# Row sums of a 64 MiB tensor: two blocks of 112 and 16 rows a partition in place of four of 32

## The chip, the cores and the metric

The kernel runs on one core of one Trainium2 chip. The metric is the device time of one execution in microseconds (us). The profile's span is a little shorter than that time: about 1.8 us lie outside the span.

## The reference

```python
def setup_inputs():
    batch, seq, dim = 32, 512, 1024
    return {"x": np.random.randn(batch, seq, dim).astype(np.float32)}

def reference(x):
    return np.sum(x, axis=-1).astype(np.float32)
```

16,384 rows of 1,024 floats are summed. 67.1 MB come in, 64 KiB go out. Nothing is used twice.

## The kernel before

Each block of 128 x n rows is laid out so that a partition holds n consecutive rows. A load tile takes 16 rows a partition: 64 KiB in each of 128 partitions, 8 MiB in all, in one of three buffers. VectorE sums whole tiles. A finished block of 32 rows a partition is stored from ScalarE's queue. The last two tiles are tuned: ScalarE takes 6 rows of the seventh, and the eighth comes in ever smaller pieces, so that little is left to do when the last bytes land. The cut below leaves lines out at each `...`, and its comments are added here.

```python
BLOCKS = (32, 32, 32, 32)
G = 16
ACT_ROWS = 6
CUT = 640
...
    xpool = ctx.enter_context(tc.tile_pool(name="x", bufs=3))
...
    def block(r0, n):
        x_b = x_flat[r0 : r0 + P * n].rearrange("(p c) d -> p (c d)", p=P)
        out_b = out_flat[r0 : r0 + P * n].rearrange("(p c) -> p c", p=P)
        return x_b, out_b, rpool.tile([P, n], F32, name=f"res{r0}")
...
        while c < whole:
            m = min(G, whole - c)
            xt = xpool.tile([P, G * D], F32, tag="xt", name="xt")
            nc.sync.dma_start(out=xt[:, 0 : m * D], in_=x_b[:, c * D : (c + m) * D])
            a = ACT_ROWS if final and c + m == whole else 0
            rows_dve(xt, res, 0, m - a, c)             # VectorE, tensor_reduce
            rows_act(xt, res, m - a, a, c + m - a)     # ScalarE, one activation a row
            c += m
        if not final:
            nc.scalar.dma_start(out=out_b, in_=res)
...
    # the eighth tile: pieces of 8, 4, 2 and 1 rows, then 640 and 384 columns of the last row
    for i, k in zip(cuts, cuts[1:]):
        nc.sync.dma_start(out=xt[:, i * D : k * D], in_=x_b[:, (c + i) * D : (c + k) * D])
    last = (n - 1) * D
    nc.sync.dma_start(out=tail[:, 0:CUT], in_=x_b[:, last : last + CUT])
    nc.sync.dma_start(out=tail[:, CUT:D], in_=x_b[:, last + CUT : last + D])
... # VectorE and ScalarE share the pieces
    nc.sync.dma_start(out=out_b, in_=res)
```

Of the kernel before, what the change touches and what calls it, by code (L numbers as in the profile page):

```python
# [1 line left out]

# [4 lines left out]

F32 = mybir.dt.float32
ADD = mybir.AluOpType.add
COPY = mybir.ActivationFunctionType.Copy  # L10
X = mybir.AxisListType.X

BLOCKS = (32, 32, 32, 32)
G = 16
ACT_ROWS = 6
CUT = 640


@with_exitstack
def kernel(  # L20
    ctx: ExitStack,
    tc: tile.TileContext,
    x: bass.AP,
    out: bass.AP,
):
    nc = tc.nc
    P = nc.NUM_PARTITIONS

    x_flat = x.flatten_outer_dims()
    R, D = x_flat.shape  # L30
    C = R // P
    assert R % P == 0 and sum(BLOCKS) == C
    out_flat = out.rearrange("a (b c) -> (a b c)", c=1)

    xpool = ctx.enter_context(tc.tile_pool(name="x", bufs=3))
    rpool = ctx.enter_context(tc.tile_pool(name="res", bufs=1))
    tail = rpool.tile([P, D + 2], F32, name="tail")

    def rows_dve(xt, res, j, n, c):
        nc.vector.tensor_reduce(  # L40
            out=res[:, c : c + n],
            in_=xt[:, j * D : (j + n) * D].rearrange("p (j d) -> p j d", d=D),
            axis=X,
            op=ADD,
        )

    def sum_act(v, acc):
        nc.scalar.activation(out=v, in_=v, func=COPY, accum_out=acc)  # L48

    def rows_act(xt, res, j, n, c):  # L50
        for i in range(n):
            sum_act(xt[:, (j + i) * D : (j + i + 1) * D], res[:, c + i : c + i + 1])

    def row_pairs_dve(xt, res, j, c):
        h = D // 2
        a, b = xt[:, j * D : j * D + h], xt[:, j * D + h : (j + 1) * D]
        nc.vector.tensor_tensor_reduce(  # L57
            out=a, in0=a, in1=b, scale=1.0, scalar=0.0, op0=ADD, op1=ADD,
            accum_out=res[:, c : c + 1],
        )  # L60

    def block(r0, n):
        x_b = x_flat[r0 : r0 + P * n].rearrange("(p c) d -> p (c d)", p=P)
        out_b = out_flat[r0 : r0 + P * n].rearrange("(p c) -> p c", p=P)
        return x_b, out_b, rpool.tile([P, n], F32, name=f"res{r0}")

    r0 = 0
    for b, n in enumerate(BLOCKS):
        x_b, out_b, res = block(r0, n)
        r0 += P * n  # L70
        final = b == len(BLOCKS) - 1
        whole = n - G - (n % G if final and n % G else 0) if final else n
        c = 0
        while c < whole:
            m = min(G, whole - c)
            xt = xpool.tile([P, G * D], F32, tag="xt", name="xt")
            nc.sync.dma_start(out=xt[:, 0 : m * D], in_=x_b[:, c * D : (c + m) * D])
            a = ACT_ROWS if final and c + m == whole else 0
            rows_dve(xt, res, 0, m - a, c)
            rows_act(xt, res, m - a, a, c + m - a)  # L80
            c += m
        if not final:
            nc.scalar.dma_start(out=out_b, in_=res)

    xt = xpool.tile([P, G * D], F32, tag="xt", name="xt")
    first = n - c - 8
    cuts = [0, first, first + 4, first + 6, first + 7]
    for i, k in zip(cuts, cuts[1:]):
        nc.sync.dma_start(out=xt[:, i * D : k * D], in_=x_b[:, (c + i) * D : (c + k) * D])
    last = (n - 1) * D  # L90
    nc.sync.dma_start(out=tail[:, 0:CUT], in_=x_b[:, last : last + CUT])
    nc.sync.dma_start(out=tail[:, CUT:D], in_=x_b[:, last + CUT : last + D])

    for i, k in zip(cuts[:2], cuts[1:3]):
        h = (k - i + 1) // 2
        rows_dve(xt, res, i, h, c + i)
        rows_act(xt, res, i + h, k - i - h, c + i + h)
    i = cuts[2]
    rows_dve(xt, res, i, 1, c + i)
    rows_act(xt, res, i + 1, 1, c + i + 1)  # L100
    row_pairs_dve(xt, res, i + 2, c + i + 2)
    nc.vector.tensor_reduce(  # L102
        out=tail[:, D : D + 1], in_=tail[:, 0 : CUT // 2], axis=X, op=ADD
    )
    sum_act(tail[:, CUT // 2 : CUT], tail[:, D + 1 : D + 2])
    nc.vector.tensor_reduce(  # L106
        out=res[:, n - 1 : n], in_=tail[:, CUT : D + 2], axis=X, op=ADD
    )
    nc.sync.dma_start(out=out_b, in_=res)


# [1 line left out]
_INS = ['x']  # L113
_OUTS = [((32, 512), 'float32')]


# [23 lines left out]
```

## Time and profile before

| before | |
|---|---|
| time | 163.21 us (median of 3 timed runs, 163.21 to 163.22) |
| the profiled execution | 163.75 us, span 162.0 us |
| mean load rate over the span | 415 GB/s |
| VectorE busy | 76% of the span |
| a tile of 8 MiB | lands every 19.33 to 19.72 us |
| VectorE's sum of a tile | 17.22 us |

The timeline of before (start in us, duration in us, engine, line and operation, then in brackets how long the engine had been idle and what ended that; lines left out). SPq and ACTq are the queues of SyncE and ScalarE, L40 is VectorE's sum:

```profile
22.68 17.22 DVE L40 TENSOR_REDUCE res<-xt 128x16 f32<-128x16384 f32 x1 [22.68 <-DMA xt<-in_x_dram]
42.04 17.22 DVE L40 TENSOR_REDUCE res<-xt 128x16 f32<-128x16384 f32 x1 [2.14 <-DMA xt<-in_x_dram]
61.56 17.22 DVE L40 TENSOR_REDUCE res<-xt 128x16 f32<-128x16384 f32 x1 [2.30 <-DMA xt<-in_x_dram]
81.28 17.22 DVE L40 TENSOR_REDUCE res<-xt 128x16 f32<-128x16384 f32 x1 [2.50 <-DMA xt<-in_x_dram]
...
122.25 0.33 SPq L91 DMA_DIRECT2D tail<-in_x_dram  x1
...
137.69 1.28 ACT L48 ACT_TABLE_LOAD   x1 [137.69 <-DVE res L40]
139.34 1.06 ACT L48 ACTIVATE xt<-xt 128x1024 f32<-128x1024 f32 x1 [0.37 <-DMA xt<-in_x_dram]
139.34 18.46 DVE L40 TENSOR_REDUCE res<-xt 128x10 f32<-128x10240 f32 x4 [2.11 <-DMA xt<-in_x_dram]
...
149.09 1.06 ACT L48 ACTIVATE xt<-xt 128x1024 f32<-128x1024 f32 x1 [3.41 <-DMA xt<-in_x_dram]
...
158.58 0.47 ACT L48 ACTIVATE tail<-tail 128x320 f32<-128x320 f32 x1 [0.97 <-DMA tail<-in_x_dram]
158.58 0.49 DVE L102 TENSOR_REDUCE tail<-tail 128x1 f32<-128x320 f32 x1
```

VectorE waits for a load before every tile, so the start of a sum is the moment its tile landed. The kernel is a load stream with work hidden under it. From 139.34 us on VectorE has no gap until 158.55 us, and at 158.58 us the next-to-last piece of the input lands: in the tail the load stream and VectorE are tied.

The chain of waits of before, and its stores in the DMA view (KB each, us from issue to landing):

```profile
by line: DMA xt<-in_x_dram 39.1%; DMA tail<-in_x_dram 22.4%; DVE res L40 21.3%; DMA out_dram<-res 14.6%; DVE res L106 0.3%; ACT tail L48 0.3%; issue 0.1%; ACTq L135 0.1%
...
98.53 23.70 DMA out_dram<-res
122.23 0.02 issue
122.25 36.30 DMA tail<-in_x_dram
```

```profile
out_dram<-res ACTq DMA_DIRECT2D x3, 16.0 KB, 23.7
out_dram<-res SPq DMA_DIRECT2D x1, 16.0 KB, 1.4
```

A store is 14.6% of the critical chain. SyncE's queue had waited 2.6 us for this store before it issued the load at 122.25 us. The two share no tile; that they share a semaphore is the likely reason, and no view names it. That load lands 36.3 us later, because it stands behind other loads: it was issued far too early for the wait to matter. A chain of waits shows what was waited for last, not what an earlier end would bring.

A second source is used below, the trace's packet records: one entry with start, duration and size for each DMA packet. They are given in plain words and tables, as no view prints them one by one. A load packet is one partition's 64 KiB. Of the 896 in before, most took exactly 2.418 us. That is 65,536 B / 2.418 us = 27.1 GB/s for an engine and 434 GB/s for sixteen. The Trainium skill (DMA: Bandwidth & Descriptors, Bandwidth, "Where 436 GB/s comes from") gives 435.2 GB/s as the ceiling of the sixteen ports; this trace agrees to half a per cent. Eight such packets for each engine and tile are 19.34 us. The stream has no room below that.

### The profile page before, as it was taken

Reading aid. Unit: us, or ns where it says so; the run is one execution under the profiler, and the core shown is the slowest. Engines: PE = TensorE matmul, PEld = TensorE weight load, DVE = VectorE, ACT = ScalarE, POOL = GpSimd, SP = SyncE. Lnnn points to the kernel's source line nnn. Section 1 sums busy time; section 2 is a strip of 40 time slices with the busy share of each in tenths; the row PEclk is TensorE's granted clock in tenths of the full one; section 3 lists DMA queues with packets and bytes.
Section 4 is the critical chain, followed back from the end, with each engine's and each line's share of the span. In section 5 each row is a group of like instructions: output and inputs, shape, how many; then the busy total and the mean of one; then the engine's idle time right before and its main releaser. Section 6 shows DMA issues by size and latency. Waiting matters only on the chain.

```text
span 162.0 us, 116 instructions
## 1 busy us (share of the span) xinstructions
DVE 123.5 (76%) x14; ACT 15.8 (10%) x29; POOL 0.2 (0%) x4
## 2 busy tenths in 40 slices
DVE  0000039998699967999499994999949998599994
ACT  0000000000000000000000000000000000991881
POOL 0000000000000000000000000000000000000000
DMA  7979989989979969969959959969969959999991
GB/s 259 518 324 453 518 356 421 518 388 388 518 340 437 518 275 502 519 259 519 519 259 518 518 259 518 519 259 519 519 260 518 518 259 518 389 398 443 405 410 35
DMA packets 2448, 67.18 MB, mean 415 GB/s; under 512 B 784, under 2 KB 912, under 8 KB 1168
## 3 DMA queue, kind: packets, MB, share of 16 engines
q1 hardware_dynamic: 2016, 67.13, 96.6%
q10 hardware_dynamic: 432, 0.05, 0.2%
HBM read 67.11 MB, written 0.07 MB: 415 GB/s over the span
## 4 chain that ended last, share of the span: by engine, by line
DMA 76%; DVE 22%; ACT 0%; issue 0%; ACTq 0%
DMA xt<-in_x_dram 39%; DMA tail<-in_x_dram 22%; DVE res L40 21%; DMA out_dram<-res 15%; DVE res L106 0%; ACT tail L48 0%; ACTq L135 0%
## 5 line engine op out<-in xcount | busy, mean ns | idle before, releaser
L40 DVE TENSOR_REDUCE res<-xt 128x16 f32<-128x16384 f32 (+4 forms) x10 | 121.8, 12203 | 36.0 <-DMA xt<-in_x_dram 36.0
L48 ACT ACT_TABLE_LOAD x1 | 1.3, 1283 | 137.7 <-DVE res L40 137.7
L48 ACT ACTIVATE xt<-xt 128x1024 f32<-128x1024 f32 x13 | 13.6, 1045 | 4.7 <-DMA xt<-in_x_dram 4.7
L48 ACT ACTIVATION_READ_ACCUMULATOR xt<-xt 128x1 f32 x13 | 2.4, 186 | 0.0
L57 DVE CUSTOM_DVE_ANT_0 xt<-xt 128x512 f32<-128x512 f32 x1 | 0.7, 693 | 0.1
L106 DVE TENSOR_REDUCE res<-tail 128x1 f32<-128x386 f32 x1 | 0.6, 554 | 0.1
L48 ACT ACTIVATE tail<-tail 128x320 f32<-128x320 f32 x1 | 0.5, 469 | 1.0 <-DMA tail<-in_x_dram 1.0
L102 DVE TENSOR_REDUCE tail<-tail 128x1 f32<-128x320 f32 x1 | 0.5, 486 | 0.0
L48 ACT ACTIVATION_READ_ACCUMULATOR tail<-tail 128x1 f32 x1 | 0.2, 187 | 0.0
L124 POOL MEMSET const-bfloat16-1.0<- 128x1 bf16 x1 | 0.1, 102 | 0.0
L124 POOL MEMSET const-uint8-127<- 128x1 uint8 x1 | 0.1, 101 | 0.0
L124 POOL MEMSET const-float32-0.0<- 128x1 f32 x1 | 0.1, 99 | 0.2 <-issue 0.2
L124 POOL MEMSET const-float32-1.0<- 128x1 f32 x1 | 0.1, 98 | 0.0
L57 DVE DVE_READ_ACCUMULATOR2_ANT res<- 128x1 f32 x1 | 0.1, 83 | 0.0
## 6 DMA issues: line engine op xcount, KB each, us to landing
xt<-in_x_dram SPq DMA_DIRECT2D x1, 4096.0 KB, 31.2
xt<-in_x_dram SPq DMA_DIRECT2D x1, 2048.0 KB, 35.7
xt<-in_x_dram SPq DMA_DIRECT2D x1, 1024.0 KB, 37.7
xt<-in_x_dram SPq DMA_DIRECT2D x1, 512.0 KB, 38.5
tail<-in_x_dram SPq DMA_DIRECT2D x1, 320.0 KB, 36.3
tail<-in_x_dram SPq DMA_DIRECT2D x1, 192.0 KB, 36.4
xt<-in_x_dram SPq DMA_DIRECT2D x7, 41.2
out_dram<-res ACTq DMA_DIRECT2D x3, 16.0 KB, 23.7
```

The source lines that it names most:

```text
L40: nc.vector.tensor_reduce(out=res[:, c : c + n], in_=xt[:, j * D : (j + n) * D].rearrange("p (j d) -> p j d", d=D), axis=X, op=ADD,)
L48: nc.scalar.activation(out=v, in_=v, func=COPY, accum_out=acc)
L57: nc.vector.tensor_tensor_reduce(out=a, in0=a, in1=b, scale=1.0, scalar=0.0, op0=ADD, op1=ADD, accum_out=res[:, c : c + 1],)
L102: nc.vector.tensor_reduce(out=tail[:, D : D + 1], in_=tail[:, 0 : CUT // 2], axis=X, op=ADD)
L106: nc.vector.tensor_reduce(out=res[:, n - 1 : n], in_=tail[:, CUT : D + 2], axis=X, op=ADD)
L124: nc = _bacc.Bacc("TRN2", target_bir_lowering=False, num_devices=1)
```

## The change

The intent is to have fewer stores while loads run: one of 112 values a partition (448 B) and one of 16 at the end, in place of four of 32. Three things come with it. The store of the large block can go only after the seventh tile, near the end. It stands in ScalarE's queue in front of the tail's row sums. And the distance in memory between the rows of neighbouring partitions, the pitch, grows from 32 rows (128 KiB) to 112 rows (448 KiB), with 64 KiB for the last tile.

```diff
-BLOCKS = (32, 32, 32, 32)
+BLOCKS = (112, 16)
...
-        whole = n - G - (n % G if final and n % G else 0) if final else n
+        whole = n - G if final else n
...
-            a = ACT_ROWS if final and c + m == whole else 0
+            a = ACT_ROWS if done + c + m == full else 0
...
-    first = n - c - 8
-    cuts = [0, first, first + 4, first + 6, first + 7]
+    cuts = [0, 8, 12, 14, 15]
```

`done` counts the rows of earlier blocks and `full` is 128 - G. The helper that sums the last single row in pairs is rewritten and renamed, but emits the same instruction; the rest of the diff is bookkeeping.

More of the change, by code (lines that the diff above doesn't have):

```diff
@@ L52, in rows_act, with pairs_dve @@
             sum_act(xt[:, (j + i) * D : (j + i + 1) * D], res[:, c + i : c + i + 1])
-    def row_pairs_dve(xt, res, j, c):
-        h = D // 2
-        a, b = xt[:, j * D : j * D + h], xt[:, j * D + h : (j + 1) * D]
+    def pairs_dve(xt, a, b, first, acc):
+        h = (a + b) // 2
         nc.vector.tensor_tensor_reduce(
-            out=a, in0=a, in1=b, scale=1.0, scalar=0.0, op0=ADD, op1=ADD,
-            accum_out=res[:, c : c + 1],
+            out=xt[:, a:h], in0=xt[:, a:h], in1=xt[:, h:b], scale=1.0, scalar=first,
+            op0=ADD, op1=ADD, accum_out=acc,
         )
@@ L65, in block @@
         return x_b, out_b, rpool.tile([P, n], F32, name=f"res{r0}")
-    r0 = 0
+    full = C - G
+    done = 0
     for b, n in enumerate(BLOCKS):
-        x_b, out_b, res = block(r0, n)
-        r0 += P * n
+        x_b, out_b, res = block(done * P, n)
         final = b == len(BLOCKS) - 1
-        whole = n - G - (n % G if final and n % G else 0) if final else n
+        whole = n - G if final else n
         c = 0
@@ L83 @@
             nc.scalar.dma_start(out=out_b, in_=res)
+        done += n
     xt = xpool.tile([P, G * D], F32, tag="xt", name="xt")
-    first = n - c - 8
-    cuts = [0, first, first + 4, first + 6, first + 7]
+    cuts = [0, 8, 12, 14, 15]
     for i, k in zip(cuts, cuts[1:]):
@@ L100 @@
     rows_act(xt, res, i + 1, 1, c + i + 1)
-    row_pairs_dve(xt, res, i + 2, c + i + 2)
+    i += 2
+    pairs_dve(xt, i * D, (i + 1) * D, 0.0, res[:, c + i : c + i + 1])
     nc.vector.tensor_reduce(
```

## The prediction

> **What bounds the kernel now.** The load stream. The page's mean is 415 GB/s over the 162.0 us span. The timeline shows when each 8 MiB tile lands, by the start of the reduce that waits for it: 22.68, 42.04, 61.56, 81.28, 100.61, 120.01, 139.34 us, every 19.33 to 19.72 us. In the trace's packet records a 64 KiB load packet takes 2.418 us at best, so 8 packets per engine and tile need 19.34 us: the steady state has no slack to win. VectorE needs 17.22 us a tile and waits 2.1 to 2.5 us for each (timeline); the next load is always queued. Only the tail is tied: from the seventh landing (139.34) VectorE runs without a gap to 158.55, when the first tail piece lands (158.58).
>
> **What the change does.**
> 1. Removes two of three mid-kernel stores (issued near 59 and 98 us). On the DMA engines each is 128 packets of 128 B, 13 ns each in the packet records: 8 per engine, about 0.1 us; the tile interval with only a store extra was 19.40 against 19.33 us. The 23.7 us from issue to landing is turn-taking with 64 KiB load packets, as the Trainium skill (DMA: Bandwidth & Descriptors, Queues, rings and completion order) has it: engines alternate between queues packet by packet; 9 store packets behind 9 of 2.42 us make 21.8 us, which agrees. The store's share of the critical chain (15%) is a semaphore reuse by a load issued long before it was needed, so worth nothing. Gain: 0.15 to 0.2 us.
> 2. Moves the remaining store. It now waits for the seventh tile's reduce (landing + 10.82 us, about 150.1) and stands in ScalarE's in-order queue ahead of the four rows of the 4 MiB piece, which started at 149.09 before. ScalarE starts them at about 150.5 (issue 0.36 us), 1.4 us late. It had idle times of 0.61, 0.30 and 0.97 us (timeline) to come, so it ends the last row about 0.4 us before the tail piece lands. Cost: 0, with small slack.
> 3. Changes the address pitch between partitions of a load from 128 KiB to 448 KiB, and 64 KiB for the last tile. The intervals 19.52 and 19.72 us hold packets of 2.45 to 2.53 us; about 0.55 us lost, not tied to stores. The skill (same page, Latency and other measured facts) reports a loss for pitches of large powers of two; 448 KiB is none, so I expect no loss. No trace here shows it yet.
> 4. The final store shrinks from 128 to 64 B per partition: its 1.4 us to landing stays. The pair-sum helper is the same instruction. The activation table load (1.28 us) moves to the start, into idle time.
>
> **Critical path.** About 0.2 us of removed DMA time lies on it, plus or minus packet luck of 0.5 us.
>
> **Prediction.** 163.0 us, range 162.3 to 163.8. Faster by over 2%: 0.02; within 2%: 0.95; slower by over 2%: 0.03.
>
> **What would show it.** Landing intervals of 19.33 to 19.5 us for all tiles (1, 3); ScalarE starting its four rows at landing + 11.2 us and still waiting for the tail piece (2); the store landing by about 156 us.
>
> **What would make it wrong.** The new pitch slowing load packets above 2.5 us on average; ScalarE's late start ending past the tail piece's landing; the late store delaying the tail loads by over 1 us; a load waiting for the late store through a shared semaphore.

## The result

After takes 163.25 us (median of 4 runs, 163.07 to 163.32) against 163.22 us (163.21 to 163.27) for before in the same rounds. The ratio is 1.0, with a 95% interval of 0.9982 to 1.0017: the same. Ratios here and below are the mean time of one kernel's fast runs over that of the other's of the same rounds, so they are not quite the ratio of the medians that are quoted.

The timeline of after, the lines that answer to those of before:

```profile
22.61 17.22 DVE L40 TENSOR_REDUCE res<-xt 128x16 f32<-128x16384 f32 x1 [22.61 <-DMA xt<-in_x_dram]
41.96 17.22 DVE L40 TENSOR_REDUCE res<-xt 128x16 f32<-128x16384 f32 x1 [2.13 <-DMA xt<-in_x_dram]
61.31 17.22 DVE L40 TENSOR_REDUCE res<-xt 128x16 f32<-128x16384 f32 x1 [2.13 <-DMA xt<-in_x_dram]
80.65 17.22 DVE L40 TENSOR_REDUCE res<-xt 128x16 f32<-128x16384 f32 x1 [2.12 <-DMA xt<-in_x_dram]
...
119.08 0.45 SPq L90 DMA_DIRECT2D tail<-in_x_dram  x1
...
138.70 18.46 DVE L40 TENSOR_REDUCE res<-xt 128x10 f32<-128x10240 f32 x4 [2.13 <-DMA xt<-in_x_dram]
138.77 1.28 ACT L48 ACT_TABLE_LOAD   x1 [138.77 <-DMA xt<-in_x_dram]
140.06 1.06 ACT L48 ACTIVATE xt<-xt 128x1024 f32<-128x1024 f32 x1
...
149.61 0.37 ACTq L82 DMA_DIRECT2D out_dram<-res  x1
150.10 1.06 ACT L48 ACTIVATE xt<-xt 128x1024 f32<-128x1024 f32 x1 [3.70 <-DVE res L40]
...
157.33 0.69 DVE L56 CUSTOM_DVE_ANT_0 xt<-xt 128x512 f32<-128x512 f32 x1 [0.16 <-DMA xt<-in_x_dram]
...
158.03 0.47 ACT L48 ACTIVATE tail<-tail 128x320 f32<-128x320 f32 x1 [0.54 <-DMA tail<-in_x_dram]
```

Its chain of waits by line, and its stores in the DMA view:

```profile
by line: DMA xt<-in_x_dram 50.5%; DMA tail<-in_x_dram 24.1%; DVE res L40 21.3%; SPq L88 1.0%; DVE res L106 0.3%; ACT tail L48 0.3%; issue 0.3%; SPq L76 0.2%; ACTq L135 0.1%
```

```profile
out_dram<-res ACTq DMA_DIRECT2D x1, 56.0 KB, 6.5
out_dram<-res SPq DMA_DIRECT2D x1, 8.0 KB, 1.4
```

Four readings. The tiles land every 19.34 to 19.36 us, the floor that the packets set. The store has left the chain, the tail load goes out 3.2 us earlier, and the time is the same: those 14.6% were worth nothing. ScalarE now starts the rows of the 8-row piece at 150.10 us, after it issued the store, 11.40 us after the seventh landing; before it was 149.09 - 139.34 = 9.75 us. And the profile of after is 0.5 us shorter (161.5 against 162.0 us) where the timed runs are equal, so something in the profile of before is chance or a tail of its distribution.

To keep the parts apart, two stretches are compared from here on, both read from the timeline: from the first landing to the seventh (six tiles in steady flow), and from the seventh landing to the start of the sums over `tail`, when the piece of 640 columns has landed.

| | first to seventh landing | seventh landing to tail piece |
|---|---|---|
| before | 139.34 - 22.68 = 116.66 us | 158.58 - 139.34 = 19.24 us |
| after | 138.70 - 22.61 = 116.09 us | 158.03 - 138.70 = 19.33 us |

### The profile page after: what moved, and what is told of

Its sections match the earlier page's. It is cut to its first block, busy times and chain, and to the rows that moved or that the text cites. A ratio compares the mean times of both kernels' runs of the same rounds, so it can differ in the third digit from the quotient of the medians.

```text
span 161.5 us, 115 instructions
## 1 busy us (share of the span) xinstructions
DVE 123.5 (76%) x14; ACT 15.6 (10%) x29; POOL 0.2 (0%) x4
## 4 chain that ended last, share of the span: by engine, by line
DMA 75%; DVE 22%; SPq 1%; ACT 0%; issue 0%; ACTq 0%
DMA xt<-in_x_dram 51%; DMA tail<-in_x_dram 24%; DVE res L40 21%; SPq L88 1%; DVE res L106 0%; ACT tail L48 0%; SPq L76 0%; ACTq L135 0%
## 5 line engine op out<-in xcount | busy, mean ns | idle before, releaser
L48 ACT ACT_TABLE_LOAD x1 | 1.3, 1283 | 138.8 <-DMA xt<-in_x_dram 138.8
L56 DVE CUSTOM_DVE_ANT_0 xt<-xt 128x512 f32<-128x512 f32 x1 | 0.7, 691 | 0.2 <-DMA xt<-in_x_dram 0.2
L56 DVE DVE_READ_ACCUMULATOR2_ANT res<- 128x1 f32 x1 | 0.1, 81 | 0.0
```

The lines of the kernel that those rows point to most:

```text
L48: nc.scalar.activation(out=v, in_=v, func=COPY, accum_out=acc)
L56: nc.vector.tensor_tensor_reduce(out=xt[:, a:h], in0=xt[:, a:h], in1=xt[:, h:b], scale=1.0, scalar=first, op0=ADD, op1=ADD, accum_out=acc,)
```

## The experiments

Theory A is that of the prediction: the load stream alone sets the time, a mid-kernel store costs 0.1 us or less, the pitch costs nothing. The rivals: B, the pitch changes the load rate, and the profiled 0.5 us is real. C, the stores disturb the stream by 0.3 us or more each, and the tail gives that gain back. D, ScalarE, held up behind the late store, gives it back. Later a theory E came out of the second stretch: the late store's packets delay the tail loads among which they run. The twelve runs below were made on three chips, those of one group on the same chip with shared runs of before.

### The kernel before again (e1_before_again)

No edit.

> The kernel before, unchanged. Theory A (the load stream alone sets the time, a store costs about 0.1 us of DMA time, the pitch nothing): its timed runs are 163.2 us; the profile of before (162.0 us of span, 163.75 us) was one unlucky execution, so a second profile has a span near 161.4 us and tile intervals of 19.34 to 19.45 us. Rival B (the profiled 0.5 us between before and after is real: slow load packets belong to the 128 KiB pitch): the second profile again shows a span near 162.0 us and intervals of 19.5 to 19.7 us.

163.25 us (6 runs, 163.06 to 163.79), ratio to before 0.9999 (0.9980 to 1.0018). Its profiled execution took 163.06 us with a span of 161.3 us. Three of its lines, the first landing, the seventh and the tail piece:

```profile
22.50 17.22 DVE L40 TENSOR_REDUCE res<-xt 128x16 f32<-128x16384 f32 x1 [22.50 <-DMA xt<-in_x_dram]
...
138.68 18.46 DVE L40 TENSOR_REDUCE res<-xt 128x10 f32<-128x10240 f32 x4 [2.14 <-DMA xt<-in_x_dram]
...
157.89 0.47 ACT L48 ACTIVATE tail<-tail 128x320 f32<-128x320 f32 x1 [0.97 <-DMA tail<-in_x_dram]
```

The first stretch is 116.18 us and the second 19.21 us. So of the 0.57 us that before seemed to lose against after in steady flow, 0.48 us (116.66 - 116.18) belong to that one execution, and this profile is the fair one to compare with: after gains 0.09 us in the first stretch and loses 0.12 us in the second.

### No mid-kernel stores (e2_no_mid_stores)

```diff
-        if not final:
-            nc.scalar.dma_start(out=out_b, in_=res)
```

Three quarters of the output stay unwritten.

> The kernel before without its three mid-kernel stores (three quarters of the output stay unwritten: wrong on purpose). Theory A: 3 x 0.1 us less, 162.9 us, every tile interval 19.34 to 19.36 us. Rival C (stores disturb the load stream by 0.3 us or more each, and the change gave that gain back in its tail): 162.3 us or less.

163.29 us (6 runs, 163.16 to 163.55), ratio 0.9998 (0.9979 to 1.0017); stretches 116.16 and 19.22 us. Rival C falls: 0.9 us or more of gain would lie outside the interval. Theory A's 0.3 us fell short too: the point estimate is 0.0002 x 163.3 = 0.03 us. The interval is 0.3 us wide on either side, so 0.3 us is only just inside. Its intervals were 19.32 to 19.41 us, not all at the floor as expected: this profile (163.39 us) has some slow load packets, of which more below. So this run bounds the stores' worth and doesn't measure it.

### The pitch alone (e3_pitch_alone)

The kernel after, with results in tiles of 32 columns that are stored when they are full:

```diff
+            if c % 32 == 0:
+                part = rpool.tile([P, 32], F32, name=f"part{c}")
-            rows_dve(xt, res, 0, m - a, c)
-            rows_act(xt, res, m - a, a, c + m - a)
+            rows_dve(xt, part, 0, m - a, c % 32)
+            rows_act(xt, part, m - a, a, c % 32 + m - a)
             c += m
-        if not final:
-            nc.scalar.dma_start(out=out_b, in_=res)
+            if not final and (c % 32 == 0 or c == whole):
+                lo = (c - 1) // 32 * 32
+                nc.scalar.dma_start(out=out_b[:, lo:c], in_=part[:, 0 : c - lo])
```

> The kernel after with its 448 KiB pitch, but results stored in column blocks of 32, 32, 32 and 16 at the times of before: the pitch alone, with one store more than before. Theory A: 163.3 us, 0.1 us above before for the fourth store and nothing for the pitch. Rival B (the pitch moves the rate of the loads): off before by 0.4 us or more, with 64 KiB load packets whose mean differs from 2.42 us.

```profile
22.48 17.22 DVE L40 TENSOR_REDUCE part<-xt 128x16 f32<-128x16384 f32 x1 [22.48 <-DMA xt<-in_x_dram]
...
138.64 10.82 DVE L40 TENSOR_REDUCE part<-xt 128x10 f32<-128x10240 f32 x1 [2.08 <-DMA xt<-in_x_dram]
...
149.97 1.06 ACT L48 ACTIVATE xt<-xt 128x1024 f32<-128x1024 f32 x1 [4.99 <-issue]
...
157.89 0.47 ACT L48 ACTIVATE tail<-tail 128x320 f32<-128x320 f32 x1 [0.54 <-DMA tail<-in_x_dram]
```

163.22 us (6 runs, 163.12 to 163.34), ratio 0.9992 (0.9976 to 1.0009); stretches 116.16 and 19.25 us. The pitch of 448 KiB doesn't move the rate: 64 KiB packets after the first sixteen averaged 2.419 us, as in e1_before_again (2.419 us). Set beside after (116.09 us), the same pitch with the early stores costs 0.07 us more in steady flow. That is what the two stores that fall in this stretch are worth. The other two fall in the second stretch: the third, as in before, and a fourth of 64 B a partition after the seventh tile. ScalarE is held behind the fourth as it is in after (its rows start 149.97 - 138.64 = 11.33 us after the landing), and yet the stretch is 0.08 us shorter than in after.

### One block, pitch 512 KiB (e4_one_block)

```diff
-BLOCKS = (112, 16)
+BLOCKS = (128,)
```

> The kernel after with BLOCKS = (128,): pitch 512 KiB, a power of two, no store before the last one, which writes 512 B per partition. Theory A with the Trainium skill's remark on large powers of two as a possible addition: without any pitch loss 163.0 us (0.2 us of late store gone, ScalarE no longer held, final store 0.1 us longer). If the pitch costs the 3% that the page's 207 against 214 GB/s suggests, 167 to 168 us with tile intervals near 20 us. Rival B expects a clear change here, A alone none.

163.8 us (6 runs, 163.62 to 164.13), ratio 1.0032 (1.0014 to 1.0050): a clear 0.5 us slower than before, where theory A expected 163.0 and the 3% of the Trainium skill's page (DMA: Bandwidth & Descriptors, Latency and other measured facts) would have been 167 to 168, an estimate. Neither was met. The first landing came late, the later intervals were as short as ever:

```profile
23.08 17.22 DVE L40 TENSOR_REDUCE res<-xt 128x16 f32<-128x16384 f32 x1 [23.08 <-DMA xt<-in_x_dram]
42.41 17.22 DVE L40 TENSOR_REDUCE res<-xt 128x16 f32<-128x16384 f32 x1 [2.10 <-DMA xt<-in_x_dram]
61.76 17.22 DVE L40 TENSOR_REDUCE res<-xt 128x16 f32<-128x16384 f32 x1 [2.13 <-DMA xt<-in_x_dram]
```

The stretches are 116.08 and 19.19 us. So it is 0.4 to 0.6 us at the start. The edit also makes the last store longer (512 B a partition), which e11_pitch_512 below keeps apart.

### The kernel after again (a1_after_again)

No edit.

> The kernel after, unchanged, a second time. Theory A: 163.1 to 163.3 us, ratio to before within 0.1% of 1; ScalarE's idle time before its tail piece again about 0.5 us. Rival C (a real gain of 0.5 us hidden by chance in the first runs): 162.8 us or less.

163.26 us (5 runs, 163.22 to 163.28), ratio 1.0 (0.9986 to 1.0015). Stretches 116.11 and 19.34 us, ScalarE's idle time before the tail piece 0.54 us again. The result stands in a second group, on another chip than the group above.

### The large store from SyncE's queue (e5_store_on_sp and e8_store_on_sp_again)

```diff
-            nc.scalar.dma_start(out=out_b, in_=res)
+            early = out_b, res
...
     nc.sync.dma_start(out=tail[:, CUT:D], in_=x_b[:, last + CUT : last + D])
+    nc.sync.dma_start(out=early[0], in_=early[1])
```

> The kernel after with the 112-row store issued from the SP queue behind the tail loads, so it no longer stands in ScalarE's queue. Theory A (ScalarE's late start is absorbed by slack): ScalarE starts the rows of the 4 MiB piece when it lands, about 1 us earlier against the seventh landing, and the time stays at 163.2 us within 0.1. Rival D (the held-up ScalarE gives back what the removed stores won): 0.2 to 0.5 us faster than after.

```profile
138.68 18.46 DVE L40 TENSOR_REDUCE res<-xt 128x10 f32<-128x10240 f32 x4 [2.13 <-DMA xt<-in_x_dram]
...
157.89 0.47 ACT L48 ACTIVATE tail<-tail 128x320 f32<-128x320 f32 x1 [0.96 <-DMA tail<-in_x_dram]
```

163.14 us (5 runs, 163.10 to 163.21), ratio 0.9994 (0.9980 to 1.0008). The stretches are 116.08 and 19.21 us. All five runs are below all five of a1_after_again on the same chip; the medians differ by 0.12 us, and so does the second stretch (19.34 - 19.21 = 0.13). That is less than rival D's 0.2 to 0.5 and more than theory A's nothing. But the edit does two things: ScalarE is no longer held, and the store's packets come behind the tail loads, in the same queue, in place of among them.

> e5_store_on_sp once more, as the base of the next three runs. Its five runs were 163.10 to 163.21 us against 163.22 to 163.28 of after on the same chip, and the stretch from the seventh landing to the tail piece 19.21 against 19.34 us. If that is real: again 163.1 to 163.2 us and 19.21 us.

On a third chip: 163.19 us (6 runs, 163.03 to 163.46), ratio 0.9987 (0.9972 to 1.0002), second stretch 19.19 us. The stage is repeated; the lead over before is not clear of noise in either group.

### Held, but no store among the loads (e9_hold_no_store)

As e5_store_on_sp, with ScalarE made to wait where the store was:

```diff
             early = out_b, res
+            sum_act(res[:, n - G : n - G + 1], spare[:, 0:1])
```

> As e5_store_on_sp (store on SP behind the tail loads), but ScalarE is still held: where the store stood in its queue it now copies one column of the seventh tile's result, for which it waits until VectorE is done. Theory E (the 0.12 us that after loses in its tail are the store's 448 B packets, 8 x 25 ns = 0.2 us per DMA engine, among the tail loads): 19.21 us from the seventh landing to the tail piece and 163.15 us. Theory D (they come of holding ScalarE): 19.33 us and 163.25 us.

The timeline of this run, the hold and the two ends of the second stretch:

```profile
138.78 18.46 DVE L41 TENSOR_REDUCE res<-xt 128x10 f32<-128x10240 f32 x4 [2.12 <-DMA xt<-in_x_dram]
...
149.63 0.20 ACT L49 ACTIVATE res<-res 128x1 f32<-128x1 f32 x1 [3.15 <-DVE res L41]
...
157.99 0.47 ACT L49 ACTIVATE tail<-tail 128x320 f32<-128x320 f32 x1 [0.79 <-DMA tail<-in_x_dram]
```

ScalarE starts the piece's rows at 149.84 us, 11.06 us after the seventh landing: it is held. The second stretch is 19.21 us all the same: holding ScalarE costs the tail nothing. The total was 163.31 us (6 runs, 163.18 to 163.45), which is 0.12 us above e8_store_on_sp_again; with runs that overlap (163.03 to 163.46) this total alone decides nothing.

### Not held, but a store among the loads (e10_store_on_pool)

```diff
-            nc.scalar.dma_start(out=out_b, in_=res)
+            nc.gpsimd.dma_start(out=out_b, in_=res)
```

> The kernel after with the same store at the same moment, issued from GpSimd's queue: its packets still run among the tail loads, ScalarE is not held. Theory E: 19.33 us from the seventh landing to the tail piece, about 163.25 us. Theory D: 19.21 us and 163.15 us. The DMA path of that queue is another one, so a store that lands at another time would spoil the test.

```profile
138.77 18.46 DVE L40 TENSOR_REDUCE res<-xt 128x10 f32<-128x10240 f32 x4 [2.14 <-DMA xt<-in_x_dram]
...
150.21 0.66 POOL L82 DMA_DIRECT2D out_dram<-res  x1 [149.76 <-DVE res L40]
...
157.39 0.69 DVE L56 CUSTOM_DVE_ANT_0 xt<-xt 128x512 f32<-128x512 f32 x1 [0.16 <-DMA xt<-in_x_dram]
...
158.12 0.47 ACT L48 ACTIVATE tail<-tail 128x320 f32<-128x320 f32 x1 [0.97 <-DMA tail<-in_x_dram]
```

ScalarE is free (its four rows started when their piece landed, at 148.56 us), and the second stretch is 19.35 us; VectorE waits 0.16 us for a load at L56, as in after. The time is 163.43 us (6 runs, 163.32 to 163.56), ratio 1.0. The store landed 5.7 us after its issue, in the same few microseconds as in after (6.5), so the test holds. Its packets are not quite those of after, though: 16 of 3,584 B, 0.15 us for an engine in place of 0.2. Together the two runs settle it for theory E: the loss in the tail follows the store's packets, not ScalarE.

Each of these stretches is one profile, so the scatter matters. In the nine profiles whose store packets in this stretch, if any, run among those of the 8-row piece or behind the last loads (before, e1, e2, e4, e5, e7, e8, e9, e11) the second stretch is 19.19 to 19.24 us; in the three with the whole late store (after, a1, e10) it is 19.33 to 19.35; with the 64 B store of e3_pitch_alone, 0.09 us an engine, it is 19.25. The packet records show where the time goes. From the end of the last packet of the 4-row piece to that of the 2-row piece, between which the late store's packets run, it is 2.59 us in after and a1_after_again and 2.61 in e6_after_2_rows and e10_store_on_pool, against 2.45 to 2.50 in the other ten profiles.

Not every store packet in that stretch costs as much. The third store of before lies in it too (in e1_before_again from 140.2 to 148.1 us, among the packets of the 8-row piece, 0.10 us an engine), and with it the stretch is 19.21 us, without it in e2_no_mid_stores 19.22.

### Two row sums more on ScalarE (e6_after_2_rows, e7_before_2_rows)

In both kernels, ahead of the piece's own rows; the sums go to a spare tile and the result stays right:

```diff
+        if i == 0:
+            rows_act(xt, spare, h, 2, 0)
         rows_act(xt, res, i + h, k - i - h, c + i + h)
```

> The kernel after with two row sums more on ScalarE (1.04 us each, 2.08 us) behind the store and before the rows of the 4 MiB piece; the result stays right. Theory A with the 0.54 us of idle time that the profile shows before the tail piece: 2.08 - 0.54 = 1.5 us slower, 164.7 us. If ScalarE's chain has no bearing on the end, 163.2 us; if it was already on the critical path, 2.1 us slower, 165.3 us.

164.62 us (5 runs, 164.48 to 164.69), ratio 1.0082 (1.0065 to 1.0099). VectorE's last sum now waits for ScalarE:

```profile
159.98 0.56 DVE L109 TENSOR_REDUCE res<-tail 128x1 f32<-128x386 f32 x1 [1.55 <-ACT tail L49]
```

> The kernel before with the same two row sums more at the same place. Its idle times of 0.61, 0.30 and 0.97 us (1.88 us) come after them: 2.08 - 1.88 = 0.2 us slower, 163.4 us. Beside e6_after_2_rows this measures how much slack the moved store takes: about 1.3 us. If the store takes none, both slow down alike.

163.43 us (6 runs, 163.14 to 163.88), ratio 1.0013 (0.9995 to 1.0031). Its tail piece was summed with no idle time before it:

```profile
158.53 0.47 ACT L49 ACTIVATE tail<-tail 128x320 f32<-128x320 f32 x1
```

The same 2.08 us of work cost 1.4 us in after (164.62 - 163.26) and 0.2 us, not clear of noise, in before (163.43 - 163.20). So the slack of 0.5 us in after and of nearly 2 us in before is real. ScalarE's hold is free in this kernel, but it used up 1.1 us of what the tail had in reserve by these times (1.36 - 0.23), 1.3 us by the idle times (1.88 - 0.54).

### Pitch 512 KiB, all else as in e5 (e11_pitch_512)

```diff
-        x_b = x_flat[r0 : r0 + P * n].rearrange("(p c) d -> p (c d)", p=P)
-        out_b = out_flat[r0 : r0 + P * n].rearrange("(p c) -> p c", p=P)
+        c0 = r0 // P
+        x_b = x_flat.rearrange("(p c) d -> p (c d)", p=P)[:, c0 * D : (c0 + n) * D]
+        out_b = out_flat.rearrange("(p c) -> p c", p=P)[:, c0 : c0 + n]
```

> As e5_store_on_sp, but partition p takes rows 128 p to 128 p + 127: pitch 512 KiB for every load (and 512 B for the two stores), nothing else changed. e4_one_block was 0.6 us slower than before; its first tile landed at 23.08 us in place of 22.5 to 22.7, with tile intervals as short as elsewhere. If the pitch does that in the first packets: first landing near 23.0 us, intervals of 19.33 to 19.36 us, 163.6 us. If it came of the long last store or of chance: first landing 22.6 us, 163.15 us.

163.63 us (6 runs, 163.48 to 163.71), all above all six of e8_store_on_sp_again on the same chip (163.03 to 163.46); the medians differ by 0.44 us. The first landing:

```profile
23.01 17.22 DVE L40 TENSOR_REDUCE res<-xt 128x16 f32<-128x16384 f32 x1 [23.01 <-DMA xt<-in_x_dram]
```

It lands at 23.01 us (23.08 in e4_one_block); in the twelve profiles with other pitches it was 22.48 to 22.91, the 22.91 being the slowest of that kernel's six runs. The stretches are 116.10 and 19.20 us. So a pitch of 512 KiB costs about 0.4 us once, at the start. In the packet records the slowest engine's first packet ended 5.72 us after the start of the span here and 5.80 in e4_one_block, against 5.20 to 5.63 elsewhere. Why the start alone suffers is open.

### The spread of the runs, over all groups

| kernel | pitch | early stores | runs | at or above 163.5 us | highest |
|---|---|---|---|---|---|
| before, in the first result and the three groups | 128 KiB | yes | 37 | 10 | 163.97 |
| e1_before_again | 128 KiB | yes | 6 | 1 | 163.79 |
| e2_no_mid_stores | 128 KiB | no | 6 | 1 | 163.55 |
| e3_pitch_alone | 448 KiB | yes | 6 | 0 | 163.34 |
| after, a1_after_again | 448 KiB | no | 9 | 0 | 163.32 |
| e5, e8, e9 | 448 KiB | no | 17 | 0 | 163.46 |

At 128 KiB now and then an execution takes some 0.5 us longer; at 448 KiB none of 32 did in these rows. It is not the chip: on each of the three chips before had 3 or 4 such runs of 11, and the kernels with 448 KiB none. (The profiled execution of before, 163.75 us, is not among its timed runs and not counted. e6, e7 and e10 are left out, as their edits move the time by themselves.) The profiles tie it to load packets: in steady flow 64 KiB packets averaged 2.430 us in the slow profiles (before, 163.75 us, and e7_before_2_rows, 163.71 us) and 2.419 to 2.420 us in the fast ones, those with a pitch of 512 KiB (2.421 to 2.422) and e2_no_mid_stores (2.425) aside. Over an engine's 55 packets after its first, 0.010 us each makes 0.55 us. That it goes with the pitch and not with the stores rests on e3_pitch_alone (stores, no slow run in 6) and e2_no_mid_stores (no stores, one in 6, and packets of 2.425 us), which is thin; what makes the packets slow is open.

## Why the prediction was right

The predicted time was 163.0 us with a range of 162.3 to 163.8; 163.25 us came out, and "within 2%" had been given 0.95. The mechanism was right: the load stream sets the time, the removed stores weigh little, and the store in the critical chain is worth nothing. Point by point:

1. **Removed stores: right in kind, about double in size.** "Gain: 0.15 to 0.2 us." The gain was 0.07 to 0.09 us (first stretch: e3_pitch_alone 116.16 and e1_before_again 116.18, after 116.09). The two intervals of e1_before_again in which a store was under way are indeed longer, 19.43 and 19.42 us against 19.31 to 19.36 us for the other four, so a store costs its interval about 0.07 to 0.1 us, as costed. Over the six tiles less than twice that remained. Part of the cost was won back: the interval behind a store was 19.30 or 19.31 us in three of the four cases of e1 and e3 (19.36 in the fourth), against 19.34 to 19.36 us for every interval of after. Why is open. The turn-taking between queues, for which the prediction named the Trainium skill (DMA: Bandwidth & Descriptors, Queues, rings and completion order), agrees at a second point: among the tail's smaller load packets the store landed in 6.5 us in place of 23.7.
2. **"Cost: 0, with small slack": the slack was right, the zero was not.** ScalarE started its rows 11.40 us after the landing where 11.2 was told, and had 0.54 us left where 0.4 was told; e9_hold_no_store shows that the hold is free, e6_after_2_rows that the slack is real. What the step left out is the store's packets. They are larger now (448 B take 25 ns in the packet records, 128 B took 13), 8 for each engine, 0.2 us, and they fall among the loads of the tail, where the stream and VectorE are tied. That cost 0.12 us (19.33 against 19.21 us), shown by e9 and e10. It cancels the gain of point 1: -0.09 + 0.12 = +0.03 us, far below what timed runs resolve here.
3. **Pitch: right for the mean.** No loss at 448 KiB. The 0.55 us in the profile of before were not tied to stores, as was said; they were those of an occasional slow execution. That the new pitch would make these rarer was not foreseen.
4. **Final store: right** (1.4 us to landing in both). **Table load: wrong, without effect.** "The activation table load (1.28 us) moves to the start" – it did not. It waited until 138.77 us, for the same landing as the first row sum behind it, and so ScalarE began that sum at 140.06, 1.36 us after the landing. This cost nothing because ScalarE then waited 3.70 us for VectorE. In before the earlier stores in ScalarE's queue had, by accident, let it run before the landing: in e2_no_mid_stores, which is before without them, it ran at 138.90 us, 0.07 us after the landing.

None of the conditions named as making it wrong came about: after's 64 KiB packets averaged 2.420 us in steady flow, the late rows ended before the tail piece landed, and no load waited for the late store, which landed at 149.61 + 6.5 = 156.1 us (156 had been told).

Of the versions tried, e5_store_on_sp is the best by median in its groups: 0.12 us below after, no overlap on the chip where both ran. Against before its ratio was 0.9994 and 0.9987, both intervals holding 1, so no version beat before beyond noise. The floor leaves little: eight tiles of 19.34 us are 154.7 of the 161.4 us of span.

## What to carry to other kernels

When a stream already runs at the rate of its packets, count what a store takes on the DMA engines (packets an engine times the packet's duration), and ask less how many stores there are than where their packets fall: in steady flow, and even among the first and largest piece of the tail, 0.1 us of them was nearly free; among the last small pieces, where the stream and the compute engine are tied, 0.15 to 0.2 us of them cost 0.12 to 0.14 us; and issued behind the last load on the loads' own queue they cost that stretch nothing. A wait in the critical chain that belongs to a transfer issued long before it is needed is worth nothing. And before a difference between two profiles is explained, see whether each profiled execution lies within the timed runs of its kernel: here half a microsecond of it did not.

## What the Trainium skill lacked or had wrong

- DMA: Bandwidth & Descriptors, Bandwidth: it has no table of the time of one packet on one engine for transfers from the SP and ACT queues. Here, in the packet records (median ns): stores of 64 B 11, 128 B 13, 448 B 25; loads of 1,536 B 65, 2,560 B 102, 4,096 B 159, 8,192 B 309, 16 KiB 611, 32 KiB 1,213, 64 KiB 2,418. From 128 and 448 B: (25 - 13) / 320 = 0.0375 ns a byte and about 8 ns for each packet.
- The same page, Latency and other measured facts: its row on pitch tells of copies within HBM, 207 GB/s at a pitch of 512 KiB where 214 is full. For loads into SBUF with runs of 64 KiB, 512 KiB cost nothing in steady flow (intervals of 19.32 to 19.39 us) but 0.4 us in the first tile; and 128 KiB showed slow executions (12 of 49 at or above 163.5 us) that 448 KiB did not (0 of 32).
- The same page, SWDGE vs HWDGE vs iDMA: it tells that a packet can hold several descriptors and should stay under 4,096 B, but not what that does for a small store. From GpSimd's queue the store of 128 x 448 B went as 16 packets of 3,584 B, 146 ns each (0.15 us an engine); from the ACT and SP queues nothing was joined: 128 packets of 448 B, 25 ns each (0.2 us an engine).
- ScalarE: Activation LUTs, What ACT_TABLE_LOAD costs: its 1,283 ns agree (1,283 ns here). It doesn't say that the load can wait for the data of the first activation behind it: 138.77 us in after, right after the landing at 138.70.
